# Softmax row sums by way of DRAM into the gate, and a hybrid encoder's start in another order

## The chip, the cores and the metric

The kernel runs on one core of one Trainium2 chip. The metric is the time of one execution in microseconds (us) of device time; the kernel before was timed three times. A core has five engines that each work through a list of instructions of their own, in order: TensorE (PE in the profile, its weight loads PEld), VectorE (DVE), ScalarE (ACT), GpSimd (POOL) and SyncE (SP). They meet at semaphores. SP here issues nearly all DMAs. SBUF is the on-chip memory, 128 partitions wide; PSUM is where TensorE writes; DRAM is the memory outside.

## The reference

One layer on 2048 new frames of a prompt and 64 frames of a running stream, width 1024. Eight heads of 64 attend to chunks of 64 frames and the eight chunks before; four heads of 128 run a gated linear recurrence. The part that the change touches:

```python
def rms_norm(x, g):
    xf = x.astype(jnp.float32)
    y = xf * lax.rsqrt(jnp.mean(xf * xf, axis=-1, keepdims=True) + EPS)
    return (y * g.astype(jnp.float32)).astype(x.dtype)

def band_attention(q, k, v, rel, valid, rel_bias):
    idx = jnp.clip(rel, -REL_CLIP, REL_CLIP) + REL_CLIP
    bias = rel_bias[:, idx].astype(jnp.float32)
    s = jnp.einsum('bnqhd,bnkhd->bnhqk', q, k).astype(jnp.float32) * ATTN_SCALE + bias
    s = jnp.where(valid[None, :, None], s, NEG_INF)
    p = jax.nn.softmax(s, axis=-1).astype(v.dtype)
    return jnp.einsum('bnhqk,bnkhd->bnqhd', p, v)

def mixer_layer(x, ln_g, w_in, lb, norm_g, w_out, attn_fn, s0):
    ...
    aq, ak, av, ag, hq, hf, hi, hg = jnp.split(rms_norm(x, ln_g) @ w_in, SPLITS, axis=-1)
    ...
    o_a = attn_fn(heads(aq), k, v).reshape(B, T, W_A) * jax.nn.silu(ag)
    o_b, S = hgrn2_branch(hq, hf, hi, hg, lb, norm_g, s0)
    y = x + jnp.concatenate([o_a, o_b], axis=-1) @ w_out
    return y, k, v, S
```

All of it is float32 to the reference's precision: an operand is split into a high part of TensorE's float32r type and the rest (xh and xl for x, w[:, 0] and w[:, 1] for a weight), and a product takes three passes, high by high, low by high and high by low.

## The kernel before

The frames are cut into four super blocks of 512 (the second with the 64 sample frames, 576). For each, x tiles of 128 frames are normed (`x_tile`: ACT's sum of squares L368 and root L336/L337, DVE's scaling by root and gain L382), turned on TensorE and split into xh (ACT, L408) and xl (DVE, L412). Then 32 jobs (`JOBS`) each project x onto 128 columns of w_in (`project`, L249 by the helper `mm`): gates and values of the four recurrence heads and of four pairs of attention heads. Attention and recurrence of a group run while the next groups are projected. After the last super block comes the product with w_out (seven products for each of eight pairs of row tiles), residual, final norm and output.

The order on every engine is written out by a planner in Python (`Plan`): each piece of work is a generator that yields what it waits for by estimated times, and the main loop gives TensorE the projections and lets the other threads put their instructions in when their estimated time has come. So an estimate that changes can move instructions on all engines, and at run time an engine that waits for one instruction holds all behind it.

At the start (`program`, `first_x`) SP loads four x tiles (xr0) and four raw weights (wr0, two of them in room that K and V take later). The gain ln_in_g comes as one row of 4 KB; TensorE spreads it over 128 partitions by a product with ones (L1970, into the PSUM tile `gps`), and the scaling of the first four tiles reads it there; ACT copies it to SBUF (`g_in`) later. TensorE turns over on the identity meanwhile (`spinning`). POOL makes the high part of the first three weights (L462), DVE that of the others (L465), POOL all low parts in four pieces (L470). `project` waits by one estimated time for all low pieces. The first two jobs run on the first 256 frames and then on the second, since the second half's x tiles come later; `x_ready` holds them by half, part and four of the eight 128-blocks. `forget_bounds` makes the constants lb and oml of the recurrence with four small DVE instructions (L302 to L305).

In attention, `softmax_rows` lets TensorE make 128 rows of scores for one head (up to 640 keys), DVE add the bias and find the negated maximum (L917), and `softmax_exp` lets ACT make the exponential with its row sum (L934), DVE the reciprocal of the sum (L937) and the scaling of p by it (L938). `attend` takes two such blocks (256 frames): TensorE turns p (`p_group`), ACT and DVE split it into ph (L946, L949), TensorE multiplies by v into pv, ACT and DVE bring both heads of a pair into `mixa` (L984, L988). `mix_out` has POOL multiply mixa by the silu gate `sga` (L1090) and SP write it to DRAM (`mixd`). There are 32 such units of a pair and 256 frames. The sample frames go through `sample_a` and the same `softmax_exp`.

Of the kernel before, what the change touches and what calls it, by code (L numbers as in the profile page):

```python
# [183 lines left out]
def hymba_step(  # L184
# [71 lines left out]
    tk = {k: Tok(C, n) for k, n in dict(acc=2, s_ps=1, tr=2, pv=1, g=1, pr=PRB, ph=2, sig=2, vT=VTB, mixa=2,  # L256
# [33 lines left out]
    def forget_bounds():  # L290

        lmx = T(cst, [P, NHB], F32, "lmx")
        le = T(cst, [P, 2, NHB], F32, "le")
        dve.tensor_tensor(lmx, lbg[:, 0], lbg[:, 1], ALU.max)
        for i in range(2):
            dve.tensor_sub(le[:, i], lbg[:, i], lmx)
        t = C.dve(300)
        yield lambda: "r1" in have
        act.activation(le, le, AF.Exp)
        t = C.act(8, t)  # L300
        yield lambda: "s1" in have
        dve.tensor_add(lmx, le[:, 0], le[:, 1])  # L302
        dve.reciprocal(lmx, lmx)
        dve.tensor_mul(lb, le[:, 0], lmx)
        dve.tensor_scalar(oml, lb, -1.0, 1.0, ALU.mult, ALU.add)  # L305
        C.dve(400, t)
        have.add("bounds")
# [43 lines left out]
    def x_tile(sb, half, c, here=None, gain=None):  # L351
# [51 lines left out]
    def x_split(sb, half, c, rows, k0, tag, pt, t):  # L403
        yield "A", t
        src = pt.rearrange("p (j t) -> p j t", t=P)[:, :, :rows]
        dh = xh[:, k0 : k0 + 4, c : c + rows]
        dl = xl[:, k0 : k0 + 4, c : c + rows]
        act.copy(dh, src)  # L408
        t = C.act(512, t)
        there(sb, half, k0, 0, t)  # L410
        yield "D", t
        dve.tensor_sub(dl, src, f32(dh))  # L412
        t = C.dve(512, t)
        tk[tag].put(1, t)
        there(sb, half, k0, 1, t)
# [19 lines left out]
    def weights():  # L435


        for j, (sb, nt) in enumerate(order):
            if sb:
                yield lambda: j - 1 in w_at  # L440
                yield from tk["w"].get()
                w = w_pair()
                sp.dma_start(f32(w), wd[nt])
                t = C.dma(1024)
                w_at[j] = (w, t, t)
                continue
# [9 lines left out]
    def w_split(j, nt, raw, t, tok):  # L456
# [4 lines left out]
        if j < 3:  # L461
# [7 lines left out]
        for k in range(0, KT, 2):  # L469
            pool.tensor_sub(w[:, 1, k : k + 2], raw[:, k : k + 2], f32(w[:, 0, k : k + 2]))  # L470
            t = C.pool(320, t)
            if k == 0:
                w_at[j] = (w, th, t + 2500.0)
            if k < KT - 2:
                yield "P", t - 300.0
# [59 lines left out]
    def project(j, ranges, evac, close=True, ready=None):  # L535
# [5 lines left out]
        for off, bn in ranges:  # L541
# [359 lines left out]
    def softmax_rows(d, h, qc, spans, bcol, nk, out):  # L901
# [28 lines left out]
        yield from softmax_exp(s, nm, nk, out, t)  # L930

    def softmax_exp(s, nm, nk, out, t):
        sm = T(wk, [P, 1], F32, "sm", bufs=4)
# [18 lines left out]
    turn = dict(given=0, tr=0, ph=0)  # L952
# [39 lines left out]
    def attend(d, g0, h, prs, mixes, before, mine):  # L992
# [60 lines left out]
        if h:  # L1053
            yield from mix_out(d, mix, g0, 256, t, g0 + 256 == SUPER[d.sb][1])
# [3 lines left out]
    def attention(d):  # L1058
# [6 lines left out]
        allprs = []  # L1065
        for g0, h in units:
            prs = [[], []]
            for b in range(2):
# [5 lines left out]
                C.spawn(softmax_rows(d, h, qc, spans, 640 - nk, nk, prs[b]), 1)  # L1074
# [3 lines left out]
        for i, ((g0, h), prs) in enumerate(zip(units, allprs)):  # L1078
            C.spawn(attend(d, g0, h, prs, mixes, marks[i - 1] if i else last_mark[0], marks[i]), 1)
# [7 lines left out]
    def mix_out(d, mix, g0, n, t, last):  # L1087
        yield lambda: d.sg_n >= g0 + n
        yield "P", t
# [241 lines left out]
    def rec_block(r, off, bn, lastb):  # L1331
# [150 lines left out]
        for i, (cc, nbk, smp) in enumerate(chunks):  # L1482
# [10 lines left out]
            if i == nprc - 1:  # L1493
                new = st_p[h] = T(cst, [P, P], F32, f"stp{h}", bufs=2)
# [413 lines left out]
    def program():  # L1908


        constants()
        kroom = f32(T(pa, [P, 2, WIN + NMAX], F32R, "kd")).rearrange("p a c -> p (a c)")
        vroom = f32(T(pa, [P, 2, 9, 2, 64], F32R, "v")).rearrange("p h t s d -> p (h t s d)")
        act.dma_start(g_in[0:1], ln_in_g.rearrange("(o d) -> o d", o=1))
# [10 lines left out]
        for what, i in (("x", 0), ("x", 1), ("w", 0), ("x", 2), ("w", 1), ("x", 3), ("w", 2), ("w", 3)):  # L1925
            if what == "x":
                sp.dma_start(xr0[i], x_rows(0, i * P, P))
            else:
# [6 lines left out]
        gps = s_ps()  # L1935
        tk["g"].take()
        tk["s_ps"].take()
# [3 lines left out]
        def first_x():  # L1941
            for c in range(4):
                C.spawn(x_tile(0, c // 2, c * P, (xr0[c], landed["x", c]),
                               gps.rearrange("p a c -> p (a c)")), 0)
            yield lambda: x_there.get((0, 1, 1), (0, 0))[0] == 4
            tk["xn"].put(3, C.now)
            yield "A", C.now
            act.copy(g_in, gps.rearrange("p a c -> p (a c)"))
            tk["s_ps"].put(1, C.act(1024))
            for a in (f32(ql[64:128, 0]), f32(ql[0:64, 1])):  # L1950
                yield "P", 0.0
                pool.memset(a, 0.0)
                C.pool(300)
# [10 lines left out]
        for _ in range(4):  # L1964
            spinning()
            C.now += 400.0
            yield None

        for a in range(2):
            pe.matmul(gps[:, a], f32(ones)[0:1], g_in[0:1, a * 512 : a * 512 + 512], start=True, stop=True)  # L1970
            C.now += 1000.0
            yield None
        have.add("gain")
        for _ in range(3):
            spinning()
            C.now += 330.0
# [188 lines left out]
```

## Time and profile before

| | |
|---|---|
| time, three runs | 1252.43, 1253.24, 1253.23 us; median 1253.23 |
| time of the profiled execution | 1252.94 us |
| its span, first to last instruction | 1251.2 us |
| instructions | 21385 |
| DMA | 287.94 MB, 230 GB/s on average |
| TensorE's granted clock | 0.999 |

A row of the profile's timeline has the start and the duration in us, the engine, the line of the kernel, the operation, what it writes and reads by the program's names, partitions x elements, how many in a row are merged (x8), and in brackets the idle time of the engine just before, with what ended it. In a row of windows stand the stretch, its length, and for PE, PEld, DVE, ACT and POOL the busy time and number of instructions, then the granted clock, the DMA engines' busy share and GB/s. In a row of waits stand who waited, for whom, the us in total, how often, and the longest. In a row of groups, behind the bar, stand busy us and mean ns of one, then the idle time before them. Matmuls overlap, so a group of n takes n times their distance and one latency.

### The profile page before, as it was taken

How to read it: one execution, taken by the hardware profiler on the slowest of the kernel's cores; microseconds unless marked ns; L12 is line 12 of the kernel's file. 1: busy time of each engine (PE TensorE's matmuls, PEld its weight loads, DVE VectorE, ACT ScalarE, POOL GpSimd, SP SyncE). 2: the span in 40 equal slices, each digit the busy share in tenths (PEclk: the TensorE clock that was granted, in tenths of full speed). 3: DMA queues.
4: the chain of work that ended last, by engine and by line, in shares of the span. 5: the costliest groups of instructions: out<-in, count | busy, mean ns of one | idle time of the engine just before them, and what ended most of it. 6: DMA issues, size and time to landing. Idle time of an engine off the chain costs nothing. (4 is left out here: it accounts for less than half of the span.)

```text
span 1251.2 us, 21385 instructions
## 1 busy us (share of the span) xinstructions
PE 1237.5 (99%) x7526; PEld 1089.1 (87%) x7526; DVE 888.8 (71%) x1889; ACT 684.5 (55%) x1533; POOL 412.4 (33%) x702
## 2 busy tenths in 40 slices
PE   8999999999999999999999999999999999999997
PEld 7888888999999999998888888988888888888786
DVE  6688879766767677686576667775857476867775
ACT  6354546655556556674465556664656445643443
POOL 6766565111110110201233242133241103474543
PEclk9999999999999999999999999999999999999999
DMA  8987979666554476654777778677666665888431
GB/s 331 335 289 242 333 268 350 207 181 223 166 186 155 146 250 192 202 165 164 274 257 249 279 261 281 224 252 255 217 245 208 215 215 207 330 272 248 144 119 67
DMA packets 137956, 287.94 MB, mean 230 GB/s; under 512 B 35257, under 2 KB 79289, under 8 KB 120186
## 3 DMA queue, kind: packets, MB, share of 16 engines
q1 hardware_dynamic: 137560, 286.58, 67.7%
q8 instruction: 59, 0.97, 0.3%
q14 instruction: 47, 0.39, 0.1%
q10 hardware_dynamic: 290, 0.01, 0.0%
HBM read 195.31 MB, written 92.27 MB: 230 GB/s over the span
## 5 line engine op out<-in xcount | busy, mean ns | idle before, releaser
L249 PE MATMUL acc<-xh,w 128*128 128x512 f32 (+2 forms) x2752 | 568.7, 345 | 0.6 <-ACT xh L408 0.6
L249 PEld LDWEIGHTS acc<-xh,w 128*128 128x128 f32 x2752 | 437.7, 189 | 49.7 <-ACT xh L408 1.0
L249 PE MATMUL acc<-xl,w 128*128 128x512 f32 (+2 forms) x1376 | 292.8, 345 | 1.6 <-DVE xl L412 1.6
L249 PEld LDWEIGHTS acc<-xl,w 128*128 128x128 f32 x1376 | 220.8, 189 | 26.6 <-DVE xl L412 2.0
L946 ACT CAST ph<-tr 128x512 fp32r<-128x512 f32 (+3 forms) x176 | 87.9, 507 | 86.9 <-PE pv L249 48.9
L934 ACT ACTIVATE pr<-pr,nm 128x640 f32<-128x640 f32 (+4 forms) x132 | 100.6, 762 | 57.1 <-DVE nm L917 56.5
L470 POOL TENSOR_TENSOR w<-wraw,w 128x256 fp32r<-128x256 f32 x120 | 103.0, 886 | 55.1 <-DVE w L465 48.2
L917 DVE CUSTOM_DVE_ANT_0 pr<-s,bias 128x640 f32<-128x640 f32 (+4 forms) x128 | 94.4, 737 | 37.0 <-PE s L249 36.4
L949 DVE TENSOR_TENSOR ph<-tr,ph 128x512 fp32r<-128x512 f32 (+3 forms) x176 | 101.2, 589 | 25.9 <-ACT ph L946 25.1
L249 PE MATMUL pv<-ph,v 128*128 128x256 f32 (+2 forms) x344 | 97.7, 370 | 0.0
L253 PE MATMUL tr<-ident,pr 128*128 128x128 f32 x580 | 88.4, 272 | 0.9 <-DVE ph L949 0.5
L506 POOL TENSOR_TENSOR xn<-wraw,xn 128x256 fp32r<-128x256 f32 x48 | 39.5, 824 | 141.9 <-ACT xn L503 136.1
L988 DVE TENSOR_TENSOR mixa<-mixa,pv 64x256 f32<-64x256 f32 (+1 forms) x144 | 56.9, 395 | 35.5 <-ACT mixa L984 32.1
L1090 POOL TENSOR_TENSOR mixa<-mixa,sga 128x256 f32<-128x256 f32 (+1 forms) x36 | 28.5, 793 | 162.4 <-DVE mixa L988 150.5
L938 DVE TENSOR_SCALAR pr<-pr,sm 128x640 f32<-128x640 f32 (+4 forms) x132 | 76.3, 578 | 4.7
L253 PEld LDWEIGHTS tr<-ident,pr 128*128 128x128 f32 x580 | 69.8, 140 | 10.6 <-PE acc L249 0.8
L1527 POOL TENSOR_TENSOR k<-ob 128x512 f32<-128x512 f32 (+2 forms) x20 | 17.9, 893 | 179.9 <-ACT ob L1518 139.8
L570 ACT ACTIVATE sig<-acc 128x512 f32<-128x512 f32 (+2 forms) x64 | 32.1, 501 | 62.7 <-PE acc L249 59.9
L249 PEld LDWEIGHTS pv<-ph,v 128*128 128x128 f32 (+1 forms) x344 | 58.3, 189 | 7.0
L984 ACT COPY mixa<-pv 64x256 f32<-64x256 f32 (+1 forms) x72 | 25.2, 351 | 58.6 <-PE pv L249 54.3
L249 PE MATMUL s<-kd,q 128*128 128x320 f32 (+2 forms) x232 | 55.9, 311 | 0.4 <-DVE nm L917 0.4
L249 PE MATMUL s<-kd,ql 128*128 128x320 f32 (+2 forms) x232 | 55.5, 309 | 0.0
(324 smaller groups left out, 2134.5 us busy)
## 6 DMA issues: line engine op xcount, KB each, us to landing
w<-wd SPq DMA_DIRECT2D x96, 1024.0 KB, 5.5
wd<-w SPq DMA_DIRECT2D x32, 1024.0 KB, 7.6
wraw<-in_w_in_dram SPq DMA_DIRECT2D x30, 512.0 KB, 5.5
wod<-xn SPq DMA_DIRECT2D x28, 512.0 KB, 5.8
xn<-in_x_prompt_dram SPq DMA_DIRECT2D x23, 512.0 KB, 4.7
bias<-biasd SPq DMA_DIRECT2D x24, 320.0 KB, 5.4
carry<-kd SPq DMA_DIRECT2D x12, 512.0 KB, 7.0
carry<-v SPq DMA_DIRECT2D x12, 512.0 KB, 5.8
```

The source lines that it names most:

```text
L249: pe.matmul(out, w, x, **kw)
L253: pe.transpose(out, x, idn)
L470: pool.tensor_sub(w[:, 1, k : k + 2], raw[:, k : k + 2], f32(w[:, 0, k : k + 2]))
L506: pool.tensor_sub(f32r(st[:, c.start + 512 : c.stop + 512]), src[:, c], st[:, c])
L570: act.activation(sig[:, :bn], acc, AF.Exp, scale=-1.0)
L917: dve.tensor_tensor_reduce(s[:, :nk].rearrange("p (a c) -> p a c", a=ns), sps[:, :ns, :kn], d.bias[:, h, bcol : bcol + nk].rearrange("p (a ...
L934: act.activation(s[:, :nk], s[:, :nk], AF.Exp, bias=nm[:, 0:1], scale=-1.0, accum_out=sm)
L938: dve.tensor_scalar(s[:, :nk], s[:, :nk], sm, None, ALU.mult)
L946: act.copy(ph[:krows, 0, :wid], pt[:krows, :wid])
L949: dve.tensor_sub(ph[:krows, 1, :wid], pt[:krows, :wid], f32(ph[:krows, 0, :wid]))
L988: dve.tensor_add(mix[hs, :qn], mix[hs, :qn], pv[hs, i, :qn])
L1090: pool.tensor_mul(mix[:, :n], mix[:, :n], d.sg[:, g0 : g0 + n])
```

## The change

**Softmax.** p is no longer scaled. The exponential's row sums of a unit's two blocks go to two columns of a tile `sums` (three of them, preset to 1). A new thread `weigh` makes their reciprocals, turns the tile by DVE in 32x32 blocks (`rt`), and SP writes eight rows of 128 B to DRAM (`way`). After the second head of a pair two reads spread the 256 numbers of each head over its 64 partitions (`rr`, one buffer). `mix_out` waits for them, and POOL multiplies the gate by rr ahead of the product of mixa and gate. The sample frames still use `softmax_exp`.

**Start.** The gain comes by a DMA that spreads it over 128 partitions, between the first and the second x tile; TensorE's two products and ACT's copy go, and TensorE turns 12 times on the identity instead of 4 and 3. The memsets of two parts of ql move ahead of the first weight. POOL makes four high parts instead of three; `project` waits for each of the four low pieces apart. The x splits wait until both tiles of their half are scaled, and the small operations of `forget_bounds` wait for tile 3 instead of tile 1.

**Also.** The recurrence states at a super block's end rotate through five buffers instead of eight (`stp`).

```diff
@@ x_tile, x_split, forget_bounds @@
-        yield lambda: "s1" in have
+        yield lambda: "s3" in have
...
-            yield lambda: "gain" in have and (not half or x_there.get((0, 0, 1), (0, 0))[0] == 4)
-        g = g_in[:rows] if gain is None else gain
+            yield lambda: not half or x_there.get((0, 0, 1), (0, 0))[0] == 4
+        g = g_in[:rows]
...
+        if not sb:
+            yield lambda: f"s{2 * half + 1}" in have
         yield "D", t
         dve.tensor_sub(dl, src, f32(dh))
@@ w_split, project @@
-        if j < 3:
+        if j < 4:
             pool.tensor_copy(w[:, 0], raw)
...
-                if i == 2:
-                    yield tl
                 for kt in range(KT):
+                    if i == 2 and kt % 2 == 0:
+                        yield lambda: len(tl) > kt // 2
+                        yield tl[kt // 2]
@@ softmax_rows @@
-        yield from softmax_exp(s, nm, nk, out, t)
+        if "t" not in sums:
+            while not tk["sums"].n:
+                yield tk["sums"]
+            if "t" not in sums:
+                sums["t"] = unit_sums()
+        b = qc // P % 2
+        act.activation(s[:, :nk], s[:, :nk], AF.Exp, bias=nm[:, 0:1], scale=-1.0, accum_out=sums["t"][:, 16 * b : 16 * b + 1])
+        out.append((s, C.act(nk + 300, t)))
+
+    def weigh(d, g0, h, prs, sums, spread):
+
+        yield lambda: len(prs[0]) and len(prs[1])
+        yield "D", max(prs[0][0][1], prs[1][0][1])
+        rs = sums["t"]
+        both = rs.rearrange("p (c j) -> p c j", c=2)[:, :, 0]
+        dve.reciprocal(both, both)
+        rt = T(wk, [P, 32], F32, "rt", bufs=2)
+        dve.transpose(rt, rs)
+        t = C.dve(250)
+        tk["sums"].put(1, t)
+        yield t + 1500.0
+        uid[0] += 1
+        way = dr.tile([8, 32], F32, tag=f"way{uid[0]}", name=f"way{uid[0]}")
+        sp.dma_start(way, rt.rearrange("(b i) x -> b i x", b=8)[:, 0])
+        t = C.dma(8)
+        spread[g0, h] = way
+        if h == 0:
+            return
+        yield from tk["rr"].get()
+        rr = spread[g0] = T(wk, [P, 256], F32, "rr", bufs=1)
+        yield t + 1000.0
+        for i in range(2):
+            sp.dma_start(rr[own[i]], spread[g0, i].rearrange("(o b) x -> o (b x)", o=1).broadcast_to([64, 256]))
+        sums["at"] = C.dma(64)
@@ mix_out @@
         yield lambda: d.sg_n >= g0 + n
+        if by:
+            yield lambda: "at" in by[1]
+            yield "P", by[1]["at"]
+            rr = by[0][g0]
+            sg = d.sg[:, g0 : g0 + n].rearrange("p (c b x) -> p c b x", c=2, b=4)
+            pool.tensor_mul(sg, sg, rr.rearrange("p (b c x) -> p c b x", b=4, c=2))
+            tk["rr"].put(1, C.pool(n + 50))
         yield "P", t
         pool.tensor_mul(mix[:, :n], mix[:, :n], d.sg[:, g0 : g0 + n])
@@ program @@
-        act.dma_start(g_in[0:1], ln_in_g.rearrange("(o d) -> o d", o=1))
...
+                sp.dma_start(g_in, ln_in_g.rearrange("(o d) -> o d", o=1).broadcast_to([P, D]))
...
-            pe.matmul(gps[:, a], f32(ones)[0:1], g_in[0:1, a * 512 : a * 512 + 512], start=True, stop=True)
```

How the program's instructions move is seen at three places. First DVE at the start, before the change, from the scaling of tile 0 to that of tile 2; `s` is the PSUM tile with the gain, xn_171, xn_172 and xn_173 are x tiles 0, 1 and 2, tr and pv the turned x:

```order
L382 SCALAR_TENSOR_TENSOR xn_171<-xn_171,rstd_201,s_186 128x512 x2
L382 SCALAR_TENSOR_TENSOR xn_172<-xn_172,rstd_210,s_186 128x512
L412 TENSOR_TENSOR xl_154<-tr_215,xh_153 128x4x128
L382 SCALAR_TENSOR_TENSOR xn_172<-xn_172,rstd_210,s_186 128x512
L302 TENSOR_TENSOR lmx_188<-le_189 128x4
L303 RECIPROCAL lmx_188<-lmx_188 128x4
L304 TENSOR_TENSOR lb_81<-le_189,lmx_188 128x4
L305 TENSOR_SCALAR oml_82<-lb_81 128x4
L412 TENSOR_TENSOR xl_154<-tr_225,xh_153 128x4x128
L412 TENSOR_TENSOR xl_154<-pv_231,xh_153 128x4x128
L412 TENSOR_TENSOR xl_154<-tr_246,xh_153 128x4x128
L382 SCALAR_TENSOR_TENSOR xn_173<-xn_173,rstd_262,s_186 128x512 x2
```

And now, from the scaling of tile 1 to the end of the forget bounds; `gin` is the gain in SBUF, xn_173, xn_174 and kd are x tiles 1, 2 and 3:

```order
L382 SCALAR_TENSOR_TENSOR xn_173<-xn_173,rstd_221,gin_152 128x512 x2
L414 TENSOR_TENSOR xl_154<-tr_212,xh_153 128x4x128
L414 TENSOR_TENSOR xl_154<-tr_225,xh_153 128x4x128
L414 TENSOR_TENSOR xl_154<-pv_235,xh_153 128x4x128
L414 TENSOR_TENSOR xl_154<-g_246,xh_153 128x4x128
L382 SCALAR_TENSOR_TENSOR xn_174<-xn_174,rstd_262,gin_152 128x512 x2
L382 SCALAR_TENSOR_TENSOR kd_168<-kd_168,rstd_285,gin_152 128x512 x2
L414 TENSOR_TENSOR xl_154<-tr_297,xh_153 128x4x128
L302 TENSOR_TENSOR lmx_189<-le_190 128x4
L303 RECIPROCAL lmx_189<-lmx_189 128x4
L304 TENSOR_TENSOR lb_81<-le_190,lmx_189 128x4
L305 TENSOR_SCALAR oml_82<-lb_81 128x4
```

Both scalings of tile 1 now stand ahead of the first xl, all scalings of tiles 2 and 3 ahead of tile 2's xl, and the four small operations have moved from between the xl of tile 0 to between those of tile 2. The scaling's third operand is gin instead of s.

Second, SP at the start, before (xn and kd take x tiles, wraw, kd and v raw weights):

```order
L1927 DMA xn_171<-in_x_prompt_dram 128x1024
L1927 DMA xn_172<-in_x_prompt_dram 128x1024
L1929 DMA wraw_174<-in_w_in_dram 128x1024
L1927 DMA xn_173<-in_x_prompt_dram 128x1024
L1929 DMA wraw_175<-in_w_in_dram 128x1024
L1927 DMA kd_166<-in_x_prompt_dram 128x1024
```

And now:

```order
L1982 DMA xn_172<-in_x_prompt_dram 128x1024
L1984 DMA gin_152<-in_ln_in_g_dram 128x1024
L1982 DMA xn_173<-in_x_prompt_dram 128x1024
L1986 DMA wraw_175<-in_w_in_dram 128x1024
L1982 DMA xn_174<-in_x_prompt_dram 128x1024
L1986 DMA wraw_176<-in_w_in_dram 128x1024
L1982 DMA kd_168<-in_x_prompt_dram 128x1024
```

The gain's load of 128 rows of 1024 stands second; x tile 1 and all behind it come one load later.

Third, SP in the second super block, before (w are weights loaded back from wd, way the DRAM tiles by which V is turned, mixd the gated output, carry K and V kept for the next super block):

```order
L616 DMA out_dram<-vT_3781 64x128
L443 DMA w_3930<-wd_45_117 128x2048
L1554 DMA mixd_13_85<-ob_3841 128x320
L443 DMA w_4054<-wd_33_105 128x2048
L870 DMA carry_0_20_92<-v_581 128x2x512
L686 DMA way_4136<-vT_4122 32x4x64 x4
L443 DMA w_4184<-wd_37_109 128x2048
L690 DMA vT_4122<-way_4136 128x256
```

And now, at the same weight w<-wd_45 (rt are the turned sums, rr the reciprocals over 64 partitions):

```order
L694 DMA vT_3799<-way_3828 64x128
L620 DMA out_dram<-vT_3799 64x128
L966 DMA way_3949<-rt_3916 8x32
L445 DMA w_3954<-wd_45_117 128x2048
L1608 DMA mixd_13_85<-ob_3857 128x320
L975 DMA rr_3951<-way_3776 64x256
L975 DMA rr_3951<-way_3949 64x256
L874 DMA carry_0_20_92<-v_573 128x2x512
L445 DMA w_4116<-wd_33_105 128x2048
L690 DMA way_4186<-vT_4166 32x4x64 x4
L966 DMA way_4209<-rt_4171 8x32
L445 DMA w_4241<-wd_37_109 128x2048
```

The writes of rt stand among the weight loads, and both reads of rr behind the second write with a weight load and an output between them.

More of the change, by code (lines that the diff above doesn't have):

```diff
@@ L254, in transpose @@
         C.now += 110.0
-    tk = {k: Tok(C, n) for k, n in dict(acc=2, s_ps=1, tr=2, pv=1, g=1, pr=PRB, ph=2, sig=2, vT=VTB, mixa=2,
+    tk = {k: Tok(C, n) for k, n in dict(acc=2, s_ps=1, tr=2, pv=1, g=1, pr=PRB, ph=2, sig=2, vT=VTB, mixa=2, rr=1, sums=3,
                                      w=WBUFS, raw=RAWB, xn=XNB, kv0=1, kv1=1, rec=1, sga=2, bias0=1, bias1=1, gf=1, gi=1, gg=1,
@@ L349, in hymba_step, with x_tile @@
     x_left = {(-1, 0): True, (-1, 1): True}
-    def x_tile(sb, half, c, here=None, gain=None):
+    def x_tile(sb, half, c, here=None):
         off, bn = SUPER[sb][3][half]
@@ L990, in finish_pv, with attend @@
         return t
-    def attend(d, g0, h, prs, mixes, before, mine):
+    def attend(d, g0, h, prs, mixes, sums, spread, before, mine):
         t0 = SUPER[d.sb][0]
@@ L1934, in program @@
         spin = psum("g")
-        gps = s_ps()
         tk["g"].take()
-        tk["s_ps"].take()
         C.now = 1400.0
@@ L1963, in program @@
         C.spawn(weights(), 2)
[L1964 removed]
+        for _ in range(12):
             spinning()
[L1966 to L1976 removed]
+            C.now += 440.0
             yield None
```

49 lines of the change are left out of this document (27 added, 22 removed).

## The prediction

> **What bounds the kernel now.** I read the page's busy shares first, then the busy time by stretch of the span, then what TensorE waited for.
>
> ```profile
> PE 1237.5 (99%) x7526; PEld 1089.1 (87%) x7526; DVE 888.8 (71%) x1889; ACT 684.5 (55%) x1533; POOL 412.4 (33%) x702
> 0.00:8.40 8.40, 6.97 (x18) 4.20 (x19) 2.21 (x7) 4.57 (x10) 3.29 (x14) 1.00 0.77 286
> 8.40:16.00 7.60, 5.34 (x31) 4.66 (x31) 6.59 (x12) 5.21 (x11) 7.51 (x12) 1.00 0.91 323
> 300.00:400.00 100.00, 100.00 (x755) 96.88 (x754) 68.55 (x189) 54.82 (x138) 11.29 (x42) 1.00 0.55 171
> PE acc L249 <- DVE xl L412: 1.6, 2, 1.4
> PE tr L253 <- DVE xn L382: 0.7, 1, 0.7
> PE tr L253 <- DVE ph L949: 0.5, 1, 0.5
> PE s L249 <- DVE nm L917: 0.4, 1, 0.4
> PE tr L253 <- DVE sig L640: 0.4, 1, 0.4
> ```
>
> In the windows the first number behind the comma is TensorE's busy time: 100 of 100 us in the middle. No other engine can shorten that. The time moves only where TensorE waits: in the first 24 us, at a few places later, and behind its last matmul. The order of the output product, the last 150 us, is not touched. So **the 80-odd us that the softmax change takes off DVE are worth at most the waits they end**.
>
> **The softmax change.** Removed: 132 less 4 scalings of p and as many reciprocals.
>
> ```profile
> L938 DVE TENSOR_SCALAR pr<-pr,sm 128x640 f32<-128x640 f32 (+4 forms) x132 | 76.3, 578 | 4.7
> L937 DVE RECIPROCAL sm<-sm 128x1 f32<-128x1 f32 x132 | 20.3, 154 | 8.1 <-ACT pr L934 7.0
> 568.66 0.82 ACT L934 ACTIVATE pr<-pr,nm 128x640 f32<-128x640 f32 x1
> 590.59 0.74 POOL L1090 TENSOR_TENSOR mixa<-mixa,sga 128x256 f32<-128x256 f32 x1 [18.00 <-DVE mixa L988]
> 599.28 0.74 POOL L1090 TENSOR_TENSOR mixa<-mixa,sga 128x256 f32<-128x256 f32 x1 [1.74 <-DVE mixa L988]
> way<-vT SPq DMA_DIRECT2D x32, 8.0 KB, 3.1
> ```
>
> 128 x (0.578 + 0.154) = 94 us of DVE go; 64 reciprocals of two columns and 64 transposes of 128x32, taken at 0.16 us each from L937, bring 20 back. POOL gets 32 products of 128x256, 32 x 0.74 = 24 us on an engine 33% busy; SP gets 64 small writes and 64 reads.
>
> Is the new way to the gate in time? After the last exponential of a pair's second head come DVE's two steps (0.3), the write and the read through DRAM. A landing costs 3.1 us by the 8 KB row, and the program puts SP's read some 4.5 us behind the write: about 8 us with the queue. In the rows above the multiply with the gate starts 590.59 - 569.48 = 21 us after the exponential. So 13 us of cover for the first 256 frames; the second reads into the same buffer once POOL's first product is done, and has the 8.7 us to 599.28 for one landing. I cost it at **nothing**. Were the cover gone, POOL would stand at the gate, with the decay products of the recurrence behind it, and TensorE behind those. SP's read waits for the write's landing, with weight loads behind it; four weight buffers of 24 matmuls each (0.23 apart by the 16 in 3.79 at 31.84 below, over 5 us) cover a few us. A wait that no row prices lies between 0 and +3 us (one 3.1 us landing, uncovered); I take 0.
>
> What the relief can end are waits on DVE between 30 and 1090 us: 0.5 + 0.4 + 0.4 = 1.3 us, each behind several DVE operations. Between 0 and -1.3 I take half: **-0.65 us**.
>
> **The start.** There the order decides.
>
> ```profile
> 4.64 1.06 ACT L368 ACTIVATE ck<-xn 128x1024 bf16<-128x1024 f32 x1 [2.55 <-DMA xn<-in_x_prompt_dram]
> 6.32 1.04 ACT L368 ACTIVATE ck<-xn 128x1024 bf16<-128x1024 f32 x1
> 7.33 2.07 DVE L382 SCALAR_TENSOR_TENSOR xn<-xn,rstd,s 128x512 f32<-128x512 f32 x3 [0.75 <-issue]
> 7.39 1.04 POOL L462 CAST w<-wraw 128x1024 fp32r<-128x1024 f32 x1 [4.04 <-DMA wraw<-in_w_in_dram]
> 7.82 0.20 ACT L337 ACTIVATE rstd<-rstd 128x1 f32<-128x1 f32 x1
> 8.58 1.91 PE L253 MATMUL tr<-ident,xn 128*128 128x128 f32 x8
> 11.56 0.74 DVE L302 TENSOR_TENSOR lmx<-le 128x4 f32<-128x4 f32 x1
> 12.46 0.59 ACT L408 CAST xh<-tr 128x512 fp32r<-128x512 f32 x1 [0.71 <-PE tr L253]
> 12.94 1.06 ACT L368 ACTIVATE ck<-xn 128x1024 bf16<-128x1024 f32 x1
> 13.03 0.95 DVE L305 TENSOR_SCALAR oml<-lb 128x4 f32<-128x4 f32 x1
> 14.45 0.20 ACT L337 ACTIVATE rstd<-rstd 128x1 f32<-128x1 f32 x1
> 15.10 0.68 DVE L412 TENSOR_TENSOR xl<-tr,xh 128x512 fp32r<-128x512 f32 x1
> 15.23 1.34 PE L249 MATMUL acc<-xl,w 128*128 128x256 f32 x8 [1.39 <-DVE xl L412]
> 16.05 0.20 ACT L337 ACTIVATE rstd<-rstd 128x1 f32<-128x1 f32 x1
> 17.13 0.60 PE L253 MATMUL tr<-ident,xn 128*128 128x128 f32 x4
> 24.36 2.08 PE L249 MATMUL acc<-xh,w 128*128 128x256 f32 x16
> 26.93 0.75 DVE L1249 TENSOR_SCALAR sig<-sig,oml,lb 128x256 f32<-128x256 f32 x1 [0.21 <-ACT sig L1246]
> 27.72 0.71 DVE L1250 TENSOR_SCALAR gk<-sig 128x256 f32<-128x256 f32 x1
> 30.77 5.39 POOL L470 TENSOR_TENSOR w<-wraw,w 128x256 fp32r<-128x256 f32 x5 [0.63 <-DVE w L465]
> 31.84 3.79 PE L249 MATMUL acc<-xh,w 128*128 128x512 f32 x16
> 31.99 1.23 DVE L1352 TENSOR_TENSOR bl<-gb 128x512 f32<-128x512 f32 x1
> 33.13 1.23 DVE L1358 TENSOR_TENSOR q<-q,gq 128x512 f32<-128x512 f32 x1
> 36.63 0.68 DVE L1369 TENSOR_TENSOR k<-k,gk 128x512 f32<-128x512 f32 x1
> ```
>
> *Loads.* Tile 0 of x is there at 4.64, the first weight, two loads later, at 7.39: 1.37 us a load of 512 KB. The gain's load, second in line, moves tile 1 from about 6.0 to 7.4 and the weight to 8.8. Tile 0 no longer waits for the broadcast through TensorE and starts near 6.5 instead of 7.33, which gains nothing as tile 1 is late: its root took 8.02 - 6.32 = 1.70, so 9.1.
>
> *Scalings.* The gain now lies in SBUF, not in PSUM. Two rows show what that does: DVE's product of two SBUF operands takes 1.23 us while POOL subtracts (30.77 to 36.16), start to start 1.14, and 0.68 when POOL does little (36.63). The scaling with the gain in PSUM ran three in 2.07 beside POOL's cast at 7.39. From 8.8 on POOL splits weights without a pause. So tile 1's two scalings take 1.23 + 1.14 and end at 11.5, not 10.5 (two at 0.69).
>
> The Trainium skill, "SBUF — State Buffer", section "Who interferes with whom", says the same in general: a DVE instruction with two SBUF inputs contends with a GpSimd instruction that reads SBUF, and one with a single SBUF input does not. By that rule the scalings are slowed, as taken here; without it the start would be 2.6 us earlier, the second rival.
>
> *The chain.* Transposes of tile 1's second half 1.1 (four at 0.21, by eight in 1.91, and their latency): 12.6. Cast 0.6: 13.2. Then the roots of tiles 2 and 3, which took 14.65 - 12.94 = 1.71 and 16.25 - 12.94 = 3.31: 14.9 and 16.5. Four scalings from 14.9, one at 1.23 and three at 1.14 more: 19.6. One xl of 0.69: 20.3. Now the forget bounds: four DVE instructions of 128x4 that before stood between the xl of tile 0, at 11.56 to 13.98 = 2.4 us (they too waited for POOL): 22.7. Second xl: 23.4. L1249 and L1250, now ahead of the last two xl, 0.75 + 0.71: 24.8. Two more xl: 26.2. TensorE, held by the last transposes of tile 3 (19.7 to 20.1) with eight lows and eight highs of 0.12 behind them, reaches the second half's xl near 22 and idles some 3.5 us until the third xl at 25.5; its last four matmuls of 0.12 end near 26.75. In before, the lows of that weight begin at 24.36: **+2.4 us**. From there both programs run the same saturated order. The finer waits on the low weights and the memsets of ql, now ahead of the first weight, lie under POOL's idle 4 us and this wait: 0.
>
> **Sum.** The profiled execution took 1252.94 us (span 1251.2 and 1.7 around it). 1252.94 + 2.4 - 0.65 + 0 = 1254.7; the median of the runs is 0.29 above it, so **1255.0 us**, +0.14%. About 0.2%, 2.5 us, is what a measurement of this kernel tells from no change: it counts as the same from 1250.7 to 1255.7.
>
> **Rivals.** *The clock falls in that wait (slower).* Eight transposes at 8.58 take 1.91, 0.213 apart; four at 17.13 take 0.60, 0.11 apart, though the granted clock is shown as 1.00 in both windows. So TensorE ran at half pace until about 10.7, some 3.6 us after its work became unbroken at 7.14. Before has no idle over 1.4 us after that; the changed kernel idles about 3.5. If half pace comes back, the next 3.6 us do 1.8 us of work: +1.8, **1256.8**. It decides from an idle stretch of about 3.4 us; mine is at that edge, against it that a shorter chain breaks it off. The Trainium skill, "TensorE: Matmul & The Clock Gate", section "What's actually happening", gives one idle window of about 3.4 us for the fall and as much sustained work for the rise; before's rise agrees, no row here shows a fall.
>
> *POOL doesn't hold the scalings.* Tile 1 ends at 10.5, the roots are at 13.9 and 15.5, the scalings at 16.95, and the same chain gives 24.15: -0.2; with the relief **1252.4**.
>
> *Nor the small operations.* Four at 0.2 and L1249/L1250 at 0.7 in all save another 2.4: the chain ends at 21.8, hardly behind TensorE itself: **1250.0**, faster. The two rows of 0.74 and 0.95 for 128x4 speak against.
>
> *The scalars' way is late after all*: POOL or SP stands for one landing in a place without cover: +3, **1258**. That the p scaling remains is no rival: its 128 instructions are gone from DVE's stream.
>
> **Chances.** Forecast 0.40 (a quarter of it beyond 1255.7), clock 0.15, no hold on the scalings 0.22 (a little of it below 1250.7), no hold at all 0.13, late scalars 0.10. That gives faster 0.17, same 0.50, slower 0.33. The range of 1250.0 to 1257.6 leaves out the late scalars and half of the fast case, under 0.2; the forecast's own is 1253.7 to 1256.3.
>
> **What would show it.** TensorE's wait for DVE's xl grows from 1.6 to some 4 us, all before 27 us; the eight half-width scalings in the first 20 us last 1.1 to 1.2 us where POOL subtracts (0.69: second rival); transposes and matmuls behind that wait keep 0.12 apart (0.21: the clock); POOL's new product shows no wait for a DMA; the wait sums behind 30 us stay within 1.5 us of before. Wrong it would be if TensorE waited at new places in the middle: then the reshuffled order, not the start, sets the sign.

## The result, and the profile after

| | before | after |
|---|---|---|
| median of 4 runs each | 1253.24 us | 1275.05 us |
| lowest to highest | 1252.43 to 1254.31 | 1272.69 to 1275.74 |
| span of the profiled execution | 1251.2 us | 1273.5 us |

The ratio is 1.0172, its 95% interval 1.0158 to 1.0185: the change costs **21.8 us**. The forecast was 1255.0, its range ended at 1257.6.

The page's busy times of after, then windows of 8 and 100 us. In a window the first number is its length, then come the busy times of TensorE, its weight loads, DVE, ACT and POOL, the granted clock, the DMA engines' share and GB/s.

```profile
PE 1245.7 (98%) x7532; PEld 1093.7 (86%) x7532; DVE 831.6 (65%) x1760; ACT 682.8 (54%) x1532; POOL 439.9 (35%) x738
8.40:16.00 7.60, 5.79 (x30) 4.88 (x29) 4.95 (x7) 5.50 (x14) 6.20 (x7) 0.58 0.97 390
24.00:32.00 8.00, 6.88 (x43) 6.79 (x44) 4.26 (x8) 2.49 (x6) 4.20 (x6) 0.79 0.89 374
200.00:300.00 100.00, 98.68 (x700) 92.18 (x698) 64.91 (x151) 56.31 (x135) 25.95 (x54) 0.98 0.75 245
300.00:400.00 100.00, 99.11 (x752) 95.45 (x752) 66.69 (x183) 54.67 (x135) 15.87 (x51) 1.00 0.53 172
1100.00:1200.00 100.00, 92.82 (x398) 73.92 (x399) 67.76 (x105) 41.47 (x100) 56.73 (x67) 0.95 0.62 201
```

DVE fell from 888.8 to 831.6 us, by 57 where the sum had 74 (94 less 20). Instructions overlap a little in the profile: taking the 94 us out alone, as e6 below does, lowers DVE's busy time by 78 (to 810.7). TensorE nevertheless has 8 us more of busy time, as its granted clock is below 1.00 in places, and idles where before does not. What it waited for, longest first:

```profile
PE pv L249 <- issue: 9.2, 1, 9.2
PE acc L249 <- DVE xl L414: 2.1, 1, 2.1
PE tr L253 <- DVE xn L382: 1.9, 1, 1.9
PE pv L253 <- DVE xn L382: 1.7, 1, 1.7
PE acc L249 <- DVE slot L1744: 1.2, 1, 1.2
PE s L249 <- DVE kd L803: 0.9, 1, 0.9
PE g L253 <- DVE xn L382: 0.8, 1, 0.8
```

The three waits for xl and xn of 1.7 us and more are the start, all before 26 us. The largest is new and stands near the end. Its row names "issue", no releaser, so it has to be read from the time line of the engines there: SP, DVE and TensorE of after.

```profile
1088.00 0.45 SPq L2062 DMA_DIRECT2D xh<-wod  x1
1088.49 0.44 SPq L2062 DMA_DIRECT2D xl<-wod  x1
1088.98 1.36 SPq L2062 DMA_DIRECT2D xh<-wod  x1
1090.42 0.40 SPq L2062 DMA_DIRECT2D xl<-wod  x1
1091.32 1.43 SPq L966 DMA_DIRECT2D way<-rt  x2
...
1093.44 0.16 DVE L958 RECIPROCAL sums<-sums 128x2 f32<-128x2 f32 x1
1103.77 0.21 DVE L960 STREAM_TRANSPOSE rt<-sums 128x32 f32<-128x32 f32 x1 [10.16 <-DMA way<-rt]
1105.24 1.27 DVE L995 TENSOR_TENSOR ph<-tr,ph 128x512 fp32r<-128x512 f32 x2
...
1096.45 0.39 PE L249 MATMUL acc<-b11l,slot 128*128 128x512 f32 x1
1106.02 2.04 PE L249 MATMUL pv<-ph,v 128*128 128x512 f32 x4 [9.18 <-issue]
```

rt has two buffers. The third transpose must not write into the first until the small DMA that reads it has landed. That DMA left SP at 1091.32, behind four loads of the output weights of 1 MB each, and landed at 1103.7: **12.4 us for 1 KB**. DVE works in order, so it stood 10.16 us at a transpose of 0.21 us, with the split of p (ph) behind it that TensorE's product with v needs. TensorE then ran at half clock for a while: the window at 1100 has 0.95.

Matched matmul by matmul (the n-th one with the same operands in both traces), after is behind before by 3.3 us at 28 us, some 5 at 200, 8 at 1055, 20.6 at 1121 and 21.6 at 1198.

### The profile page after: what moved, and what is told of

It reads as the page before. It is cut to its first block, busy times and chain, and to the rows that moved or that the text cites. A ratio compares the mean times of both kernels' runs of the same rounds, so it can differ in the third digit from the quotient of the medians.

```text
span 1273.5 us, 21557 instructions
## 1 busy us (share of the span) xinstructions
PE 1245.7 (98%) x7532; PEld 1093.7 (86%) x7532; DVE 831.6 (65%) x1760; ACT 682.8 (54%) x1532; POOL 439.9 (35%) x738
## 5 line engine op out<-in xcount | busy, mean ns | idle before, releaser
L949 ACT ACTIVATE pr<-pr,nm 128x640 f32<-128x640 f32 (+4 forms) x128 | 97.3, 760 | 53.3 <-DVE nm L930 49.4
L1030 ACT COPY mixa<-pv 64x256 f32<-64x256 f32 (+1 forms) x72 | 25.1, 349 | 63.5 <-PE pv L249 58.0
L1603 POOL TENSOR_TENSOR ob<-ob,gg 128x512 f32<-128x512 f32 (+2 forms) x20 | 24.1, 1208 | 94.4 <-DVE ob L1599 91.1
```

What stands on the lines that cost most here:

```text
L949: act.activation(s[:, :nk], s[:, :nk], AF.Exp, bias=nm[:, 0:1], scale=-1.0, accum_out=sums["t"][:, 16 * b : 16 * b + 1])
L1030: act.copy(mix[hs, :qn], pv[ls, 0, :qn])
```

## The experiments

A time behind a run is its median, and "+" is its distance from the kernel before on the same chip (1252.94 to 1253.35).

### The two buffers of rt

```diff
-        rt = T(wk, [P, 32], F32, "rt", bufs=2)
+        rt = T(wk, [P, 32], F32, "rt", bufs=8)
```

> The changed kernel with 8 buffers instead of 2 for the transposed sums rt, nothing else. Theory A: DVE's transpose of the third pair waited 10.2 us for the small write way<-rt to read its old buffer, and TensorE's 9.2 us at 1106 with the half clock behind it (some 3.4 us, alignment +12.5 in all) are that wait: 1275.05 - 12.5 = about 1262.5 (1260 to 1265), no wait of rt for a DMA left. Rival B: the landing itself is late, and with the buffer free the same lateness arrives by another road, the read rr<-way and POOL's product with the decay products and the gate behind it: 1270 to 1276, with POOL waiting for rr and TensorE for POOL in place of DVE.

**1264.04, +10.69** (ratio 1.0085, 1.0070 to 1.0100): 11 us less than after. All that TensorE waits for behind 1050 us in e1 are four short waits:

```profile
PE acc L249 <- DVE slot L1744: 1.2, 1, 1.2
PE acc L249 <- DVE pr L1832: 0.6, 1, 0.6
PE acc L249 <- DVE sga L579: 0.6, 1, 0.6
PE acc L249 <- DVE xn L1832: 0.2, 1, 0.2
```

Theory A holds: half of the loss is one buffer's wait for one landing. The landing itself is as late as ever, but nobody stands for it in that place.

### One half of the change each

```diff
 e2: the diff's hunks on the start alone, on the kernel before
 e3: the diff's hunks on the softmax alone, on the kernel before
```

> The kernel before with only the change of the start (gain's row by DMA, order of the x tiles, finer waits on the low weights). Prediction's term: +2.4 us, 1255.6. By the alignment of the two traces, with the half clock behind the wait at 25: +3.3, 1256.5 (1255.8 to 1257.2). Rival: the start's loss is caught up later, as TensorE waits anyway: 1253 to 1254.

> The changed kernel with the old start: the softmax change alone. Theory A, the late landing belongs to this half: 1275.05 - 3.3 = 1271.8 (1269 to 1274), a long wait of rt for way<-rt near 1090 to 1106 again. Rival: that the transpose of the third pair falls right behind the weight loads is chance of the order and goes when the order is moved by 3 us: 1256 to 1262.

e2: **1256.31, +2.96** (1.0014 to 1.0033). e3: **1267.18, +13.83** (1.0098 to 1.0128), with TensorE's long wait again (8.8 us), for the same transpose. The rival of e3, that another order removes it, falls. Apart the two halves cost 16.8 us, together 21.8: some 5 us come only from both.

### The small writes on another queue

```diff
-        sp.dma_start(way, rt.rearrange("(b i) x -> b i x", b=8)[:, 0])
+        act.dma_start(way, rt.rearrange("(b i) x -> b i x", b=8)[:, 0])
```

> The changed kernel with the 64 small writes way<-rt issued by ACT instead of SP. If a small write is late because it stands in SP's own queue behind the weight loads of 1 MB, its landing on another queue takes some 3 us even at 1091 to 1106, DVE's wait goes and the time falls to 1260 to 1265. If all queues share the loaded DMA engines, the write lands as late as before: 1272 to 1277, and ACT, which stands for the transpose before it can issue, may add to that.

**1275.03, +21.68**: no gain. DVE no longer waits for rt (0.2 us in all); ACT stands instead. ACT's time line of e4:

```profile
1101.48 1.07 ACT L992 CAST ph<-tr 128x512 fp32r<-128x512 f32 x2
1108.18 0.55 ACTq L966 DMA_DIRECT2D way<-rt  x1
1108.83 0.37 ACT L992 CAST ph<-tr 128x256 fp32r<-128x256 f32 x1 [6.28 <-DMA xh<-wod]
```

What ended ACT's wait is a load of output weights (xh), which neither the small write nor the cast behind it uses. The program's own rows tell why; these are SP's in after, with what each waits for:

```
784 L2062 DMA xh_153<-wod_67_139 128x2048
785 L2062 DMA xl_154<-wod_67_139 128x2048 [waits DMAHW4_49]
786 L2062 DMA xh_153<-wod_68_140 128x2048 [waits DMAHW5_49]
787 L2062 DMA xl_154<-wod_68_140 128x2048 [waits DMAHW6_49]
788 L966 DMA way_12992<-rt_12954 8x32 [waits DMAHW7_49,DVE_49]
789 L966 DMA way_13043<-rt_13010 8x32 [waits DMAHW0_49,DVE_49]
```

The transfers of this program carry eight semaphores in turn, DMAHW0 to 7, on whichever queue they go. Each is issued only when the one eight places earlier has landed. So a write of 1 KB among loads of 1 MB is held before it is issued, and its issuer with it. ACT stood like this at 193 us too, 6.5 us for an x tile, and TensorE waited 3.4 us behind each of the two.

The landing itself did get shorter. By the trace's records of the semaphores, the write that ACT issued at 1097.98 landed at 1102.76, ahead of all four weight loads that SP had issued before it: 4.8 us instead of 12.4. So e4's first theory was right on the landing, where SP's own queue had been the bound, and wrong on the time: the wait moved to the issue, and the engine that issues pays.

### The softmax change in pieces

e5 is e3 with the 8 buffers. e6 is the kernel before without the prompt's scalings of p, in before's order on every engine. e9 is e5, and e10 is e1, with the way of the sums left out and the rest in place:

```diff
 e6 (before)
-        dve.reciprocal(sm, sm)
-        dve.tensor_scalar(s[:, :nk], s[:, :nk], sm, None, ALU.mult)
+        if nk == 576:
+            dve.reciprocal(sm, sm)
+            dve.tensor_scalar(s[:, :nk], s[:, :nk], sm, None, ALU.mult)
 e9, e10 (weigh and mix_out)
-        dve.reciprocal(both, both)
-        dve.transpose(rt, rs)
-        sp.dma_start(way, rt.rearrange("(b i) x -> b i x", b=8)[:, 0])
-            sp.dma_start(rr[own[i]], ...)
-            pool.tensor_mul(sg, sg, rr.rearrange("p (b c x) -> p c b x", b=4, c=2))
```

> The softmax change alone (old start) with 8 buffers for rt. If the late landing is all that this half costs, its 8.8 us of wait and the half clock behind it go: 1267.2 - 11 (what e1 saved) = 1256.2, and what is left above before's 1253.35 (about +1 by 1055 us and +1 behind 1100 in e3's alignment) is the changed order of everything else. If the two halves only cost together: 1253 or less. If the late landing comes back on another road: 1260 or more.

> The kernel before with the 128 reciprocals and scalings of p left out of the prompt's softmax (p stays unnormalised there) and nothing in their place; every other instruction stands in before's order. This is the relief of DVE by itself. Prediction's term: between 0 and -1.3 us, -0.65, so 1252.7 (1252.0 to 1253.4). Rival: DVE's 94 us open more than the waits that the trace names, 1250 or less.

> e5's kernel with the sums left unused: no reciprocal, no transpose, no write, no read and no product by the gate (the attention's output stays unnormalised), and every other instruction in e5's order. If the 4.3 us that e5 is above before are the changed order: 1257.4 again (1256.5 to 1258). If they are the way of the scalars itself (its transfers, POOL at the gate, SP): 1253.1 (1252.3 to 1254.2).

> e1's kernel (both halves of the change, 8 buffers for rt) with the same things left out and the rest in its order. The start alone costs 3.0 (e2). If the stretch at 250 to 310 us, where the traces of after and e1 lose some 4 us more than the start, is the way's doing: 1256.1 (1255 to 1257.2), the sample's x landing sooner than 9.3 us. If it is the order: 1260 to 1261, and TensorE waits at 252 and 305 as in after.

| run | median | above before | interval of the ratio |
|---|---|---|---|
| e6, relief alone | 1253.19 | +0.09 | 0.9993 to 1.0011 |
| e9, softmax's order alone | 1255.01 | +2.07 | 1.0009 to 1.0026 |
| e5, softmax with 8 buffers | 1257.45 | +4.35 | 1.0027 to 1.0052 |
| e10, start and order | 1260.22 | +7.28 | 1.0047 to 1.0073 |
| e1, start, order and way | 1264.04 | +10.69 | 1.0070 to 1.0100 |

*The relief is worth nothing that can be measured* (e6).

*The order costs by itself.* The planner, given other costs, puts all work of the middle in another order. That costs 2.1 us with the old start. With the new start, order and start cost 7.3, where 2.1 + 3.0 = 5.1 were to be had from the parts. The other 2.2 are no more than the spread of the three runs (their intervals together allow 0 to 4.5), but the traces show them at one place: matched with e9, e10 loses 3.8 us between 245 and 250 us and wins some 1 back later. It is the x of the sample, late at 250 us, in e10 as in after and e1 though e10 has no way of the sums at all. e10's rows of its tile, then TensorE's waits around:

```profile
L358 SPq DMA_DIRECT2D xn<-in_x_sample_dram x1: 579/579/579, 238.0 to 238.0; - x1
  DMA xn<-in_x_sample_dram: 2.2, 1
250.58 0.46 PE L253 MATMUL g<-ident,xn 64*128 64x64 f32 x4 [0.72 <-DVE xn L382]
252.24 0.39 PE L249 MATMUL s<-kd,q 128*128 128x256 f32 x1 [0.38 <-DVE nm L930]
254.00:256.00 2.00, 2.00 (x9) 1.90 (x8) 1.90 (x4) 2.00 (x8) 0.00 (x0) 0.50 0.18 61
```

ACT waited 2.2 us for that load, TensorE 0.72 and 0.38, and then the clock was at 0.50. For this place e10's expectation decides for the order, not for the way.

*The rest of the way costs 2 to 3 us in the middle.* Matched matmul by matmul, e5 falls behind e9 at two places only, 2.15 us at 294 and 0.94 near 430. At the first, ACT stood for the sample's cache, whose loads SP had issued behind a write and four reads of the new way; e9, without these, has ACT wait 1.73 us there, and TensorE not at all. e5's lines of ACT and TensorE:

```profile
292.54 0.62 ACT L607 CAST wraw<-ck 128x512 fp32r<-128x512 f32 x1 [4.34 <-DMA ck<-in_cache_attn_v_dram]
294.45 1.44 PE L249 MATMUL acc<-xh,w 128*128 128x320 f32 x8 [1.81 <-ACT vT L768]
```

### The way of the sums in before's order

e7 is before with the sums, transposes, writes, reads and POOL's product put in, 8 buffers for rt, and every other instruction in its old place. In e13 SP's read waits in the program until POOL's product has used rr; seven reads move. e15 is e13 with the last pair of heads in the old form.

```diff
 e7 (before)
+        act.activation(s[:, :nk], s[:, :nk], AF.Exp, ..., accum_out=two["t"][:, 16 * b : 16 * b + 1])
         t = C.dve(0.55 * nk + 150, t)
+        if two["n"] == 2:
+            dve.reciprocal(both, both)
+            dve.transpose(rt, rs)
 e13 (e7)
+        yield from tk["rr"].get()
         rr = spread[g0] = T(wk, [P, 256], F32, "rr", bufs=1)
 e15 (e13)
+        if d.sb == len(SUPER) - 1 and d.p == NPAIR - 1:
+            yield from softmax_exp(s, nm, nk, out, t, True)
+            return
```

> The softmax change (sums, transposes, writes, reads, POOL's product) with 8 buffers for rt, with every other instruction of every engine in before's order and the old start. If the new way costs nothing by itself and e5's rest is the order, as the prediction had it: e6's time, 1252.7 (1252.0 to 1253.6). If the way itself costs (SP standing for landings with the weight loads behind it, POOL at the gate, the product slowing DVE): 1255 to 1258, with waits of TensorE that before does not have.

> e7's kernel, with SP's read of a pair's sums let go only when POOL's product has used the one buffer rr; seven of the reads move behind other transfers on SP, nothing else moves on any engine. If e7's 6 us at 103 us are SP standing from 93.2 to 103.4 for that buffer with the weight loads behind it, they go: about 1258.5 (1257 to 1260). If they are POOL standing at the gate for a late landing, the read is now issued no earlier than before and 1264 to 1266 stays.

> e13's kernel with the last pair of heads in the old form (8 of the 128 reciprocals and scalings of p, no sums, no transposes, no DRAM, no product), the other 60 of 64 writes as in e13. If the way of the scalars costs only where its landings stand behind the output weights of 1 MB, behind 1080 us, e13's 6 us go and, as e6 showed no worth in DVE's relief, the time is before's: 1253.3 (1252.6 to 1254.2). If the way costs elsewhere too: 1256 or more.

e7: **1264.58, +11.48** (1.0087 to 1.0114); my expectation of no cost was wrong. 6 of it come at 103 us. SP stood from 93.2 to 103.4 for the one buffer rr, with weight loads behind it, and TensorE idled; e7's SP, then TensorE:

```profile
92.75 0.42 SPq L479 DMA_DIRECT2D wd<-w  x1
103.44 0.47 SPq L964 DMA_DIRECT2D rr<-way  x1
...
PE pv L249 <- ACT k L1510: 3.2, 1, 3.2
```

e13: **1259.36, +6.11** (1.0032 to 1.0062): that stall is gone. Matched with before, e13 is 0.2 us behind at 1054 us, 0.97 at 1101 and 5.1 at 1181. The 60 of 64 writes issued by then cost next to nothing in before's order: the cover of 13 us that the prediction counted is there. The price is at the output weights, where SP stands for landings again, and TensorE for a weight load (v) that SP issues only behind them:

```profile
1099.54 0.60 SPq L956 DMA_DIRECT2D way<-rt  x1
1102.77 5.61 SPq L965 DMA_DIRECT2D rr<-way  x2
1108.49 0.52 SPq L1138 DMA_DIRECT2D mixd<-mixa  x1
...
1117.06 0.51 PE L249 MATMUL acc<-v,slot 128*128 128x512 f32 x1 [0.76 <-DMA v<-wod]
```

e15: **1256.48, +3.29** (1.0016 to 1.0036), half of e13's loss. The expected 1253.3 was missed: the trace is level with before up to 1055 us and loses 1.7 near 1100 and 1.1 by 1180, though no way is left there. The trace shows where, but not why: near 1081 us ACT stood 3.30 us for a read of the gated output (sig<-mixd), for which it stood 1.26 in before, and TensorE waited 2.1 us behind it (before: 0.5). In e6, which has no way at all, ACT stood 2.48 us there and TensorE waited 0.6, so this read lands late without the way too. Why e15 loses more by it is open.

### The start

e8 lets the forget bounds go early again, e12 puts the gain into PSUM; both are built on e2.

```diff
 e8
-        yield lambda: "s3" in have
+        yield lambda: "s1" in have
 e12
+        if not sb and not c:
+            act.copy(g_ps.rearrange("p a c -> p (a c)"), g_in)
-        g = g_in[:rows]
+        g = g_ps.rearrange("p a c -> p (a c)")[:rows] if not sb else g_in[:rows]
```

> The change of the start alone, with the four small operations of the forget bounds let go after the first half's xl again (where before has them) instead of after the second half's first xl. Prediction's step: they cost up to 2.4 us on the chain to the second half's xl; taken back, e2's 1256.3 falls to about 1254 (1253.5 to 1255). Rival: TensorE waits for x tile 1 and the transposes instead (e2's trace shows 2.3 and 1.7 us for xn), and they cost nothing: 1255.8 to 1257.

> The change of the start alone with the gain copied by ACT (one copy of 1024 elements, about 1.0 us) into PSUM, from where the eight half-width scalings read it; else e2's order. If POOL's weight split holds the scalings when both operands lie in SBUF: 0.69 to 0.75 us each instead of 1.1 to 1.2, eight of them some 3 us less on DVE; on the chain, less the copy, 1254 to 1255.3. If the scalings are not what the start waits for: 1256 to 1257.

e8: **1255.33, +2.23**, 0.7 us less than e2, where up to 2.4 had been reckoned, and not beyond the spread of the two: the bounds are a small part at most. e12: **1253.98, +1.04** (1.0001 to 1.0019), 1.9 us less than e2. The same scalings in after, and in e12 with the gain in PSUM:

```profile
10.04 2.31 DVE L382 SCALAR_TENSOR_TENSOR xn<-xn,rstd,gin 128x512 f32<-128x512 f32 x2 [1.68 <-ACT rstd L337]
17.74 2.36 DVE L382 SCALAR_TENSOR_TENSOR kd<-kd,rstd,gin 128x512 f32<-128x512 f32 x2
...
10.27 1.41 DVE L386 SCALAR_TENSOR_TENSOR xn<-xn,rstd,s 128x512 f32<-128x512 f32 x2 [1.07 <-ACT rstd L337]
16.91 1.41 DVE L386 SCALAR_TENSOR_TENSOR kd<-kd,rstd,s 128x512 f32<-128x512 f32 x2 [0.20 <-ACT rstd L337]
```

2.31 and 2.36 us for two become 1.41, beside the same split of weights on POOL, whose four subtractions get shorter too (2.8 us, in after 3.6 and 4.2). That the scalings were held is shown by these rows. What it is worth rests on the medians alone: the intervals of e2 and e12 overlap, and their profiled executions took 1255.10 and 1254.98 us.

### The clock in the start's wait

```diff
+                    if j == 0 and off and i == 1 and kt == 0:
+                        fill = s_ps()
+                        for _ in range(32):
+                            pe.matmul(fill[:, 0, :P], ident, ident, start=True, stop=True)
```

This is e11, on e1; e14 has 9 in place of 32.

> e1's kernel with 32 idle matmuls of 128x128, into a PSUM tile that nothing reads, ahead of the matmuls that wait for the second half's xl (32 x 0.06 = 1.9 us of the 2.1 to 2.7 us wait). If TensorE's clock falls because of that idle stretch, as the prediction's clock rival has it, the granted clock from 24 to 29 us stays 1.00 where e1 and after show 0.5, and 1.7 us come back: 1262.3. If it falls for another reason, 0.5 is there again: 1264.

> e11 again with 9 idle matmuls instead of 32: e11's took 7.31 us (64 recorded, 0.114 each), far longer than the wait, and so hid the gain. Nine take 2.06 us of e1's wait of 2.7. If the idle stretch is what halves the clock, it stays at 1.00 from 25 to 29 us, and e1's 1264.0 falls by the 1.5 that e11's alignment gave back: 1262.5 (1261.5 to 1263.3). If the remaining 0.6 us of idle time still halve it: 1264.

e11: **1266.54, +13.60**, slower, and my error of size: a matmul of fp32 is recorded twice, so 32 took 7.31 us where I had reckoned 1.9, and held up the real work by 4.3 us. Yet e11 falls only 2.8 us behind e1 by 32 us. e14: **1260.97, +7.72** (1.0041 to 1.0075), 3 us less than e1, where 1.5 were expected. Windows of 1 us, after and then e14:

```profile
24.00:25.00 1.00, 0.00 (x0) 0.00 (x0) 1.00 (x3) 0.42 (x1) 1.00 (x2) 1.00 0.94 393
26.00:27.00 1.00, 1.00 (x7) 1.00 (x6) 0.98 (x1) 0.00 (x0) 1.00 (x2) 0.50 1.01 426
...
24.00:25.00 1.00, 1.00 (x12) 1.00 (x11) 1.00 (x3) 0.42 (x1) 1.00 (x3) 1.00 1.06 434
26.00:27.00 1.00, 1.00 (x11) 1.00 (x10) 0.85 (x1) 0.00 (x0) 1.00 (x2) 1.00 0.98 414
```

With TensorE kept busy in the wait, the clock stays at 1.00. The 3 us are more than this clock's share alone: near 254 us e1's clock falls to half once more, and e14's does not.

That wait is not the only place of the start where the clock falls. Above, after's window of 8.40 to 16.00 us stands at 0.58, where the prediction's row of before has 1.00. In e2's profile it comes later (behind the length: TensorE's busy time, clock, DMA share, GB/s):

```profile
8.40:16.00 7.60, 4.76 (x24) 0.73 0.98 393
16.00:24.00 8.00, 8.00 (x60) 0.83 1.01 344
```

The traces also record each change of the clock. Before's record begins only at 10.75 us, so its 1.00 ahead of that is not measured. With the new start the record begins at full clock (after: 4.56 us), the clock falls while TensorE waits for the first tiles, and it is at half from 7.98 to 14.80 us in after and from 11.89 to 18.72 in e2. All nine traces with the new start have such a spell of 3.4 or 6.8 us, and none of the eight with the old one records any. In e2 it ends last: there TensorE is 1.4 us behind before at 20 us (after is level), so it comes later to the second half's xl and waits 0.7 us for it instead of 2.1. No run has the new start without this spell, so what it costs is open.

## Why the prediction was wrong, step by step

The sum of what was found, against after's 21.8: rt's wait 11.0 (after less e1), the rest of the way 3.4 (e1 less e10, each above its own before; 1.5 of it stands before 70 us, where no way exists yet, and is the spread of the start), order and start 7.3 (e10).

- *What bounds the kernel, and that DVE's relief is worth at most the waits it ends*: right. -0.65 was forecast, e6 shows +0.09, which that measurement can't tell from it.
- *The way of the sums costs nothing, with +3 as the bound, "one 3.1 us landing, uncovered"*: **the step that failed.** By the sum above it cost up to 14.4 us (11.0 for one wait, 3.4 for the rest), and it was mis-sized twice. First, the landing. The 3.1 us were the median of 32 writes of 8 KB; the same view of before has these medians for the loads of output weights, behind which the small write landed:

```profile
xh<-wod SPq DMA_DIRECT2D x2, 1024.0 KB, 10.0
xl<-wod SPq DMA_DIRECT2D x2, 1024.0 KB, 15.0
b11l<-wod SPq DMA_DIRECT2D x1, 1024.0 KB, 12.6
```

  The small write behind them took 12.4 us. Second, who waits. I named POOL and SP. In the changed kernel it was DVE, at a transpose into a buffer that a DMA still had to read, with all of DVE's later work behind it. SP stood as well where the order was before's (e7, e13).
- *"13 us of cover"*: right in before's order up to 1054 us (e13: 0.2 us), wrong at the output weights (5.1 by 1181). It rested on one place of the middle, at 590 us.
- *"From there both programs run the same saturated order"*: wrong. The order costs 2.1 us alone, and by the medians 2.2 more together with the new start. The text's own warning, waits at new places in the middle, came true at 252 and 305 us.
- *The start, +2.4*: right in sign and about in size, +2.96 (1.8 to 4.1 by the interval). DVE's chain came out as reckoned: the third xl of the second half ends at 25.1 us in after (24.39 and 0.68), for 25.5. TensorE's waits did not: 2.1 us (0.7 in e2) for the xl instead of 3.5, and 1.9 and 1.7 before it for the scaled tiles. The spell of half clock between 8 and 19 us stood nowhere in the sum, so part of the fit in size may be luck. POOL's hold on the scalings, on which the second and third rivals turned, is there: 1.1 to 1.2 us each as announced, and e12 takes 1.9 of the 3 us back by the medians. This agrees with the rule of the Trainium skill's "SBUF — State Buffer" that the prediction cited. The forget bounds were over-sized, at most some 0.7 for up to 2.4.
- *The clock rival*: it happened in after (0.50 at 26 us), and in e2's profile only earlier, at the first tiles. It was to decide from 3.4 us of idle time; 2.1 us were enough.
- *The late-scalars rival*, at 0.10, was the right one by kind, but priced at +3, about a fifth of what it cost.

## What to carry to other kernels

Before a small transfer is called hidden, list every instruction that must wait for its landing, those that only want its source buffer back included, and price the landing by the slowest row of the place where it runs, not by the median of its size elsewhere. A queue of its own can shorten the landing (4.8 for 12.4 us here). But in a program whose transfers share a few semaphores, a small transfer also waits, before it is issued, for a large one ahead of it, on any queue. An engine's relief is worth the waits of the bounding engine that it ends, and a planner that is given new costs changes more than the edit: run the edit in the old order too, to price the two apart.

## What was not expected of the hardware

TensorE's clock fell on less idle time than thought. In after, as in e10's rows above, it idled 0.8 and 0.4 us near 252 us, with a few transposes of 64x64 and matmuls between, and then lost half its clock:

```profile
253.00:254.00 1.00, 0.62 (x6) 0.48 (x4) 0.93 (x7) 1.00 (x6) 0.00 (x0) 0.87 0.10 39
254.00:257.00 3.00, 3.00 (x13) 2.81 (x13) 2.56 (x8) 2.79 (x10) 0.00 (x0) 0.50 0.18 44
257.00:259.00 2.00, 2.00 (x16) 2.00 (x15) 1.85 (x7) 1.98 (x9) 0.00 (x0) 0.96 0.00 0
```

The shares give 0.26 us at half pace in the first window, 3.0 in the second and 0.16 in the third: 3.4 us. The Trainium skill, "TensorE: Matmul & The Clock Gate", section "What's actually happening", has the clock fall after at least one idle window of about 3.4 us. The length of the half pace agrees, the condition doesn't: 1.1 us of idle time was enough here and 2.1 at the start, while before's 1.39 us at 15 us shows no fall.

The records of the clock say more. In each of the 17 traces it changes only at the edges of a grid of 3.41 us; after's half pace here is the grid's window from 253.74 to 257.15, and in the window just before it TensorE was busy 0.67 of the time. Counted up to 1240 us, a window at full clock with TensorE busy 0.48 of it or less was followed by half clock every time (16 of 16), one above 0.73 never, and between the two 5 of 35 were. Before's window with the 1.39 us, busy 0.69, was one of the other 30. Full clock came back only behind a window that was busy 0.93 or more. So in these traces the share of a window counts, not one unbroken idle stretch, and between 0.48 and 0.73 the share alone doesn't decide. A short wait of TensorE costs itself and, now and then, 1.7 us behind it.
